# Mixer: convolution and gate tiles as pairs of seven products, the retention output product first, the sums at a phase boundary earlier

## The chip, the cores and the metric

One core of one Trainium2 chip runs one launch of the kernel. The metric is device time in microseconds of that launch; lower is better. TensorE does the matrix products, VectorE and ScalarE the elementwise work, GpSimd (POOL) a little of it and a queue of transfers, SyncE (SP) the queue of weight loads.

## The reference, cut to what matters

One inference step of a two-layer decoder trunk. 512 prompt tokens and 8 x 4 sampled tokens are taken together here: 544 columns. Each layer is a feed-forward block, a mixer, and a second feed-forward block, all with norms before and after. All arithmetic is float32. The mixer, on which the change acts:

```python
proj = u @ w_in                       # 1024 -> 512 q, 512 k, 1024 v, 1024 g, 1024 bg, 1024 cg, 1024 xc, 2048 gates
o = head_rmsnorm(retention(q, k, v, s0))
o_ret = (silu(g) * o) @ w_ret_out     # 1024 x 1024
z = w[0]*full[t] + w[1]*full[t+1] + w[2]*full[t+2]    # full = buffer of 2 rows, then cg * xc
o_conv = (bg * z) @ w_conv_out        # 1024 x 1024
gate_r, gate_c = split(sigmoid(gates))
merged = gate_r * o_ret + gate_c * o_conv
h = h + rmsnorm(merged @ w_o)
```

## The kernel before, in words

Everything is kept transposed: a tile is 128 features x 544 tokens, and 1024 features are KT = 8 tiles. Tokens are worked on in two halves of 272 columns (`hs(0)`, `hs(1)`). A float32 operand is cut into two float32r parts, high and low, and a product is three matmuls: high x high, high x low, low x high (`step`, `mm` on line 321). A *plain job* makes one output tile of 128 features: 8 input tiles x 2 halves x 3 = 48 matmuls into two banks of PSUM. Its weights come by SP's queue into `raw` (three buffers), ScalarE copies the high part (`whi`, line 249), VectorE subtracts the low one (`wlo`, line 253), into 14 buffers, so several jobs ahead.

A *pair* (`Pair`, `run_pair`) makes two output tiles at once. It sees the two weight tiles, each cut in two over its inputs, and the inputs, each tile's two halves of tokens, as 2 x 2 blocks, and does seven block products in place of eight, after a scheme of sums of blocks. A block product is 4 input tiles x 3 = 12 matmuls, so a pair is 84. It uses three banks X, Y, Z. ScalarE copies X into Y (`seed`, line 191) and Z into `p7` (line 392); VectorE forms `Z = Y + p7` (line 395) and `c22 = Y + p7` (line 403) between products, and the last product adds to Y after c22 has been read. The sums of weight blocks are `s_13`, `s_24` (lines 275 to 282, VectorE), cut into parts at lines 260 and 261. The input sums (`ops`: B11, B21, B22, T1 to T4) are made once per phase by `build_ops`, for k = 0 to 3, two feature tiles each; it multiplies x by the gain and the norm's reciprocal r, so the outputs of pairs are normalized already. Before the change, only feed-forward phases have pairs (in parts 2 to 4 of their up product; jobs at `BUILD_AT` call `build_ops`).

A mixer phase before (`mix_jobs`): four heads of six plain jobs (q, k, two v, two g), each head followed by a script of retention work that runs between the steps of later jobs (`retention`, `self.side`, `tick`); three convs of three plain jobs (cg, xc, bg); eight times a gate job (I_GR) and a ret_out job; five more convs; eight times a gate job (I_GC) and a conv_out job; eight wo jobs. The evacuation of plain jobs multiplies by r. Plain jobs' own outputs with r: `ev_gate` line 748, `ev_out` line 754, `ev_cg` 691, `ev_xc` 702, `ev_bg` 723.

The instruction order of TensorE and SP is the order of the program. VectorE, ScalarE and POOL are ordered by a scheduler's priorities, but in a *boundary* between two phases they too follow a script written by hand: `ev(t, fn)` puts fn at planned time t, in us from the start of the next phase's head, and `play` emits all in order of t. The last TAIL = 5 jobs of a phase run half 0 first, then half 1; then the norm's `ry`, the `chain` (scale y, add to x, cut x into `xh` and `xl`, lines 1090 to 1075) per half; then the *head*: the first HEAD = 5 jobs of the next phase, half 0 then half 1, whose banks are copied to SBUF (`copy`, line 1249) since the next norm's r is not known yet. The squares of x are summed into `acc` (`pre_sum`, lines 434 to 443), from planned times `SUMS` = 17.0 and 24.0 on. `rstd` makes r of a half: a matmul with ones (line 464), ScalarE's reciprocal root (476), three instructions of VectorE (477 to 479). `rest(half)` calls rstd and then the evacuations of the five head tiles; it runs from `head_side` as side work after the boundary, at HEAD_REST = 0.5 and 3.2 planned us. The retention script of head 0 begins 4 planned us after the first job behind the head, with `s_transposes` on the tile `stk` (lines 855 to 890).

Activations live in one pool of U_BUFS = 54 buffers of 544 columns (tag u). x is spilled to DRAM (`xd`) and filled again at each boundary, by POOL's queue.

Of the kernel before, what the change touches and what calls it, by code (L numbers as in the profile page):

```python
# [14 lines left out]
DM = 1024  # L15
# [17 lines left out]
BUILD_AT = (6, 9, 11, 13)  # L33
EPS = 1e-6
# [26 lines left out]
SUMS = 17.0, 24.0  # L61
URGENT = 300
HEAD_REST = 0.5, 3.2
# [52 lines left out]
class Pair:  # L116
# [9 lines left out]
    def __init__(self, w1, w2, ops, evac, after=None):  # L126
        self.w1, self.w2, self.ops, self.evac, self.after = w1, w2, ops, evac, after


class Trunk:  # L130
    def __init__(self, ctx, tc, a):
# [10 lines left out]
        self.xd = self.dp.tile([KT, P, NT], F32, tag="xd", name="xd")  # L142
        self.turn, self.given, self.taken = 0, {}, []
# [224 lines left out]
    def run_pair(self, i, j):  # L368

        nc, V = self.nc, self.nc.vector  # L370
        self.prep(i + 1)
        ahead = i + (2 if isinstance(self.jobs[i + 1], Pair) else 1 + LOOK)
# [117 lines left out]
    def ffn_jobs(self, ph):  # L490
# [76 lines left out]
        ph["ops"] = {o: [None] * (KT // 2) for o in ("B11", "B21", "B22", "T1", "T2", "T3", "T4")}  # L567
# [4 lines left out]
    def build_ops(self, ph, k):  # L572
# [5 lines left out]
        for f in (k, k + KT // 2):  # L578
            t = self.u("n")
            V.scalar_tensor_tensor(out=t, in0=self.x[f], scalar=self.gain(l, ph["pre"], f), in1=ph["r"],  # L580
                                   op0=ALU.mult, op1=ALU.mult)
            n.append(t)
            self.spill(f)
        n1, n2 = n
        b11 = self.u("b11", F32R)
        nc.scalar.activation(out=b11[:, A], in_=n1[:, A], func=AF.Copy)
        V.tensor_tensor(out=b11[:, B], in0=n1[:, A], in1=b11[:, A].bitcast(F32), op=ALU.subtract)
# [4 lines left out]
        V.scalar_tensor_tensor(out=t24[:, B], in0=t24[:, A], scalar=-1.0, in1=n2[:, A], op0=ALU.mult, op1=ALU.subtract)  # L592
        b2, p13, p24 = [self.cut((self.u("oh", F32R), self.u("ol", F32R)), t) for t in (n2, t13, t24)]
        for o, hl, s in (("B21", b2, A), ("B22", b2, B), ("T1", p13, A), ("T3", p13, B), ("T2", p24, A), ("T4", p24, B)):
            ph["ops"][o][k] = (hl[0][:, s], hl[1][:, s])
        ph["ops"]["B11"][k] = (b11[:, A], b11[:, B])

# [27 lines left out]
    def mix_jobs(self, ph):  # L625
# [59 lines left out]

        def conv(f):
# [6 lines left out]
            def ev_xc(half, ps):  # L693
                if half == 0:
                    A = st["A"] = self.u("A")
                    S = st["S"] = self.tp.tile([P, NB, 6], F32, tag="as", bufs=2, name=self.name("as"))
                    nc.gpsimd.memset(A[:, 0:2], 0.0)
                    nc.gpsimd.tensor_copy(S[:, :, 0:2], ph["sc"][:, f])
# [5 lines left out]
                if half == 1:  # L704
# [3 lines left out]
                    zs = z[:, SEQ:NT].rearrange("p (b j) -> p b j", j=TS)  # L708
                    cw = [self.cw[:, (l * 3 + i) * KT + f:(l * 3 + i) * KT + f + 1] for i in range(3)]
                    nc.scalar.activation(out=z[:, :SEQ], in_=A[:, 0:SEQ], func=AF.Copy, scale=cw[0])  # L710
                    nc.scalar.activation(out=zs, in_=S[:, :, 0:4], func=AF.Copy, scale=cw[0])
                    for i in (1, 2):
                        nc.vector.scalar_tensor_tensor(out=z[:, :SEQ], in0=A[:, i:i + SEQ], scalar=cw[i],
                                                       in1=z[:, :SEQ], op0=ALU.mult, op1=ALU.add)
                        nc.vector.scalar_tensor_tensor(out=zs, in0=S[:, :, i:i + 4], scalar=cw[i], in1=zs,
                                                       op0=ALU.mult, op1=ALU.add)
                    nc.gpsimd.tensor_copy(ph["cs"][:, f, 0:2], A[:, SEQ:SEQ + 2])
                    nc.gpsimd.tensor_copy(ph["cs"][:, f, 2:18].rearrange("p (b j) -> p b j", j=2), S[:, :, 4:6])

            def ev_bg(half, ps):  # L720
# [4 lines left out]
                if half == 1:  # L725
                    bz[f] = st["z"]
                    if f >= 3:
                        split_bz(f)
# [11 lines left out]
        def out_pair(m, wi, wo, hl, last):  # L740
            st = {}

            def ev_gate(half, ps):
                if half == 0:
                    st["g"] = self.u("gate")
                s = self.hs(half)
                g = st["g"][:, s]
                nc.vector.tensor_tensor(out=g, in0=ps[:, :HALF], in1=ph["r"][:, s], op=ALU.mult)
                nc.scalar.activation(out=g, in_=g, func=AF.Sigmoid)

            def ev_out(half, ps):
                s = self.hs(half)
                g = st["g"][:, s]
                nc.vector.tensor_tensor(out=g, in0=ps[:, :HALF], in1=g, op=ALU.mult)
                if not last:
                    rm[m] = st["g"]
                    return
                if half == 0 and (m < 3 or m == KT - 1):
                    mhl[m] = (self.u("mh", F32R), self.u("ml", F32R))
                nc.vector.tensor_tensor(out=g, in0=rm[m][:, s], in1=g, op=ALU.add)  # L760
                if m in mhl:
                    self.split(*mhl[m], st["g"], s)
                elif half == 1:
                    rm[m] = st["g"]

            return [Job(w[l, wi + m], mv, ev_gate), Job(wo[l, m], lambda: [hl[f] for f in range(KT)], ev_out)]
# [5 lines left out]
        def ready_ret():  # L772
            self.tick(drain=True)
            for f in range(KT):
                split_ret(f)

        def ready_conv():
            for f in range(3):
                split_bz(f)

        def ready_merged():
            for m in range(3, KT - 1):
# [687 lines left out]
```

## Time and profile before

| | |
|---|---|
| time, median of 3 runs | 2715.28 us (2714.5 to 2715.72) |
| the profiled execution: its own time | 2717.34 us |
| its span, first to last instruction | 2715.6 us |
| mean granted clock of TensorE | 0.994 of full speed |
| instructions | 50898 |
| moved by DMA | 283.50 MB, mean 104 GB/s |

All durations below are from the one profiled execution. The times of runs and of the profiled execution hold the launch's ends beside the span. Engines run side by side, so busy times don't add up to the span.

### The profile page before, as it was taken

The numbers are of one execution on the slowest core, as the hardware profiler recorded it, in microseconds if no ns is written. First come the engines' busy times: TensorE is split into PE (matmuls) and PEld (weight loads), VectorE is DVE, ScalarE is ACT, GpSimd is POOL, SyncE is SP. The second block draws the span as 40 slices with busy tenths as digits, with TensorE's granted clock in tenths as the row PEclk, the third lists the DMA queues.
The fourth block names the chain that finished last, engine by engine and source line by source line (L and its number), as shares of the span: only waits on it lengthen the run. The fifth ranks groups of instructions, "written<-read, shape, count | busy, mean of one in ns | idle before, by whom it ended". The sixth has DMA issues, their size and how long they took to land.

```text
span 2715.6 us, 50898 instructions
## 1 busy us (share of the span) xinstructions
PE 2671.4 (98%) x21126; PEld 2658.0 (98%) x21126; DVE 1697.5 (63%) x2995; ACT 1261.2 (46%) x2340; POOL 205.4 (8%) x327
## 2 busy tenths in 40 slices
PE   9999998999999999999999999989999999999998
PEld 9999998999999999999999999989999999999997
DVE  6855757765344368567488657577643443885673
ACT  6555554433222355555565555643432223655553
POOL 1000021121000010000100000211200001000002
PEclk9999999999999999999999999999999999999999
DMA  4233443332222332332332334433322223323332
GB/s 150 90 102 94 132 137 121 105 125 78 93 88 87 94 130 77 101 95 92 128 120 91 93 97 146 140 106 107 114 86 86 90 91 103 105 91 96 102 98 93
DMA packets 88135, 283.50 MB, mean 104 GB/s; under 512 B 11296, under 2 KB 15520, under 8 KB 87904
## 3 DMA queue, kind: packets, MB, share of 16 engines
q1 hardware_dynamic: 74592, 235.46, 28.1%
q0 software_dynamic: 13312, 44.79, 4.8%
q8 instruction: 165, 2.70, 0.4%
q14 instruction: 66, 0.54, 0.1%
HBM read 257.25 MB, written 22.95 MB: 103 GB/s over the span
## 4 chain that ended last, share of the span: by engine, by line
PE 48%; DVE 2%; DMA 1%; ACT 1%; issue 0%; DVEq 0%; ACTq 0%
PE banks L321 46%; DVE wlo L253 0%; ACT whi L249 0%; DMA raw<-in_w_down 0%; DMA raw<-in_w_up 0%; PE banks L464 0%; PE banks L1008 0%; DVE rot L644 0%; ACT sq L437 0%; PE banks L990 0%; PE banks L923 0%; PE banks L1011 0%; DMA raw<-in_w_in 0%; PE banks L969 0%; DVE yg L1119 0%
## 5 line engine op out<-in xcount | busy, mean ns | idle before, releaser
L321 PE MATMUL banks<-xh,whi 128*128 128x272 f32 x2688 | 748.6, 294 | 1.2 <-ACT whi L1313 1.2
L321 PE MATMUL banks<-xl,whi 128*128 128x272 f32 x2688 | 735.8, 289 | 0.0
L249 ACT ACTIVATE whi<-raw 128x1024 fp32r<-128x1024 f32 (+2 forms) x341 | 326.4, 957 | 698.7 <-PE banks L321 477.6
L321 PE MATMUL banks<-xh,wlo 128*128 128x272 f32 x2688 | 596.0, 289 | 0.6 <-DVE wlo L1317 0.4
L321 PEld LDWEIGHTS banks<-xh,whi 128*128 128x128 f32 x2688 | 508.6, 189 | 3.7 <-ACT whi L1313 1.6
L321 PEld LDWEIGHTS banks<-xl,whi 128*128 128x128 f32 x2688 | 508.5, 189 | 1.1
L253 DVE TENSOR_TENSOR wlo<-raw,whi 128x1024 fp32r<-128x1024 f32 (+2 forms) x341 | 374.2, 1099 | 168.9 <-ACT whi L249 143.6
L321 PEld LDWEIGHTS banks<-xh,wlo 128*128 128x128 f32 x2688 | 438.9, 189 | 1.3 <-DVE wlo L1317 0.9
L321 PE MATMUL banks<-oh,whi 128*128 128x272 f32 x1360 | 391.9, 288 | 3.1 <-ACT banks L191 3.0
L321 PE MATMUL banks<-oh,wlo 128*128 128x272 f32 x1360 | 392.1, 288 | 0.0
L321 PE MATMUL banks<-ol,whi 128*128 128x272 f32 x1360 | 390.9, 287 | 0.0
L321 PE MATMUL banks<-hh,whi 128*128 128x272 f32 x1408 | 385.2, 289 | 0.2
L321 PE MATMUL banks<-hl,whi 128*128 128x272 f32 x1408 | 384.4, 288 | 0.4 <-DVE hl L542 0.2
L321 PE MATMUL banks<-hh,wlo 128*128 128x272 f32 x1408 | 313.3, 288 | 0.0
L321 PEld LDWEIGHTS banks<-hl,whi 128*128 128x128 f32 x1408 | 264.9, 188 | 1.0 <-DVE hl L542 0.8
L321 PEld LDWEIGHTS banks<-hh,whi 128*128 128x128 f32 x1408 | 264.9, 188 | 1.0 <-ACT banks L191 0.8
L321 PEld LDWEIGHTS banks<-oh,whi 128*128 128x128 f32 x1360 | 255.8, 188 | 4.2 <-ACT banks L191 4.2
L321 PEld LDWEIGHTS banks<-ol,whi 128*128 128x128 f32 x1360 | 256.3, 188 | 0.0
L321 PEld LDWEIGHTS banks<-oh,wlo 128*128 128x128 f32 x1360 | 255.8, 188 | 0.0
L321 PEld LDWEIGHTS banks<-hh,wlo 128*128 128x128 f32 x1408 | 229.6, 188 | 0.0
L261 DVE TENSOR_TENSOR wlo<-s,whi 128x1024 fp32r<-128x1024 f32 x136 | 166.6, 1225 | 75.2 <-ACT whi L260 39.1
L260 ACT ACTIVATE whi<-s 128x1024 fp32r<-128x1024 f32 x136 | 143.4, 1054 | 41.8 <-DVE s L282 22.2
(233 smaller groups left out, 4332.4 us busy)
## 6 DMA issues: line engine op xcount, KB each, us to landing
raw<-in_w_up SPq DMA_DIRECT2D x173, 512.0 KB, 3.5
raw<-in_w_in SPq DMA_DIRECT2D x128, 512.0 KB, 3.5
raw<-in_w_down SPq DMA_DIRECT2D x96, 320.0 KB, 3.0
raw<-in_w_down SPq DMA_DIRECT2D x32, 448.0 KB, 4.1
xd<-x POOLq DMA_DIRECT2D x40, 272.0 KB, 2.6
x<-xd POOLq DMA_DIRECT2D x40, 272.0 KB, 4.9
s<-in_state_ret POOLq DMA_DIRECT2D x32, 256.0 KB, 3.5
out_ret_s<-s POOLq DMA_DIRECT2D x32, 256.0 KB, 3.0
```

Source lines behind the costliest of these rows:

```text
L249: self.nc.scalar.activation(out=hi[:, :n], in_=r[:, :n], func=AF.Copy)
L253: eng.tensor_tensor(out=lo[:, :n], in0=r[:, :n], in1=hi[:, :n].bitcast(F32), op=ALU.subtract)
L260: self.nc.scalar.activation(out=hi, in_=r, func=AF.Copy)
L261: self.nc.vector.tensor_tensor(out=lo, in0=r, in1=hi.bitcast(F32), op=ALU.subtract)
L321: self.nc.tensor.matmul(out=ps[:, :HALF], lhsT=w, rhs=x, start=start, stop=stop, skip_group_check=again)
```

## The change

The mixer's convs 0 and 1 stay plain (`CONV_PLAIN` = 2). Convs 2 to 7 and all sixteen gate tiles become 17 pairs a layer: a conv pair makes cg and xc of one conv (6), a bg pair makes bg of two convs (3), a gated pair makes the two gates of one m (8). The order of a mixer phase is now: four heads, convs 0 and 1, eight ret_out jobs, three triples (conv pair, conv pair, bg pair), eight times a gated pair and a conv_out job, eight wo jobs. The ret_out outputs are copied to SBUF, stored to a DRAM tensor `od`, and loaded again (`rm`) one gated step ahead. The mixer's ops are built after ret_out jobs 0, 2, 4, 5 (`BUILD_MIX`), with x reloaded from `xd` by POOL's queue; r is no longer multiplied in these evacuations. The splits of seven merged tiles are put together before the last conv_out job. `build_ops` forms t13 and t24 ahead of b11. At every boundary, and at the start, the sums begin earlier (`SUMS` 11.0 and 19.0, 0.45 apart in place of 0.6), one weight preparation moves from 20 to 14, rstd of the two halves is called inside the script at 17.5 and 22.5 (`RSTD_HEAD`), `rest(0)` at 22.6, and `rest(1)` and the spills right after the script.

```diff
@@ -31,6 +31,8 @@
+CONV_PLAIN = 2
+BUILD_MIX = (0, 2, 4, 5)
@@ -58,9 +60,9 @@
-SUMS = 17.0, 24.0
+SUMS = 11.0, 19.0
...
-HEAD_REST = 0.5, 3.2
+RSTD_HEAD = 17.5, 22.5
...
 def log_gammas():
@@ -369,6 +372,8 @@
+        if j.before:
+            j.before()
@@ -564,7 +569,7 @@
-        ph["ops"] = {o: [None] * (KT // 2) for o in ("B11", "B21", "B22", "T1", "T2", "T3", "T4")}
+        self.no_ops(ph)
@@ -577,23 +582,29 @@
-            V.scalar_tensor_tensor(out=t, in0=self.x[f], scalar=self.gain(l, ph["pre"], f), in1=ph["r"],
-                                   op0=ALU.mult, op1=ALU.mult)
+            if ph["kind"] == "mix":
+                nc.gpsimd.dma_start(out=t, in_=self.xd[f])
+            V.scalar_tensor_tensor(out=t, in0=t if ph["kind"] == "mix" else self.x[f],
+                                   scalar=self.gain(l, ph["pre"], f), in1=ph["r"], op0=ALU.mult, op1=ALU.mult)
...
-            self.spill(f)
+            if ph["kind"] != "mix":
+                self.spill(f)
...
-        b11 = self.u("b11", F32R)
-        nc.scalar.activation(out=b11[:, A], in_=n1[:, A], func=AF.Copy)
-        V.tensor_tensor(out=b11[:, B], in0=n1[:, A], in1=b11[:, A].bitcast(F32), op=ALU.subtract)
...
+        b11 = self.u("b11", F32R)
+        nc.scalar.activation(out=b11[:, A], in_=n1[:, A], func=AF.Copy)
+        V.tensor_tensor(out=b11[:, B], in0=n1[:, A], in1=b11[:, A].bitcast(F32), op=ALU.subtract)
...
+    def no_ops(self, ph):
+        ph["ops"] = {o: [None] * (KT // 2) for o in ("B11", "B21", "B22", "T1", "T2", "T3", "T4")}
...
     def spill(self, f):
@@ -683,6 +694,64 @@
+        def conv_tiles(f):
+            A = self.u("A")
+            S = self.tp.tile([P, NB, 6], F32, tag="as", bufs=2, name=self.name("as"))
+            nc.gpsimd.memset(A[:, 0:2], 0.0)
+            nc.gpsimd.tensor_copy(S[:, :, 0:2], ph["sc"][:, f])
+            return A, S
+        def short_conv(f, A, S, z):
...
+        def conv_pair(f):
+            st = {}
+            def ev(tile, half, c):
+                s = self.hs(half)
+                if tile == 0:
+                    if half == 0:
+                        st["c"] = self.u("cg")
+                    nc.scalar.activation(out=st["c"][:, s], in_=c, func=AF.Copy)
+                    return
+                if half == 1:
+                    st["A"], st["S"] = conv_tiles(f)
+                A, S, t = st["A"], st["S"], st["c"][:, s]
+                n = HALF if half == 0 else SEQ - HALF
+                nc.vector.scalar_tensor_tensor(out=A[:, 2 + half * HALF:2 + half * HALF + n], in0=c[:, :n], scalar=-1.0,
+                                               in1=t[:, :n], op0=ALU.mult, op1=ALU.mult)
+                if half == 1:
+                    nc.vector.scalar_tensor_tensor(out=S[:, :, 2:6], in0=c[:, n:].rearrange("p (b j) -> p b j", j=TS),
+                                                   scalar=-1.0, in1=t[:, n:].rearrange("p (b j) -> p b j", j=TS),
+                                                   op0=ALU.mult, op1=ALU.mult)
+                else:
+                    bz[f] = self.u("z")
+                    short_conv(f, A, S, bz[f])
+            return Pair(w[l, I_CG + f], w[l, I_XC + f], lambda: ph["ops"], ev)
+        def bg_pair(f):
+            def ev(tile, half, c):
+                z = bz[f + tile][:, self.hs(half)]
+                if tile == 0:
+                    nc.vector.tensor_tensor(out=z, in0=c, in1=z, op=ALU.mult)
+                else:
+                    nc.vector.scalar_tensor_tensor(out=z, in0=c, scalar=-1.0, in1=z, op0=ALU.mult, op1=ALU.mult)
+                if half != tile:
+                    split_bz(f + tile)
+            return Pair(w[l, I_BG + f], w[l, I_BG + f + 1], lambda: ph["ops"], ev)
         def conv(f):
@@ -724,8 +780,6 @@
-                    if f >= 3:
-                        split_bz(f)
@@ -737,33 +791,46 @@
-        def out_pair(m, wi, wo, hl, last):
+        def ret_out(m):
...
-            def ev_gate(half, ps):
+            def ev(half, ps):
...
-                    st["g"] = self.u("gate")
-                s = self.hs(half)
-                g = st["g"][:, s]
-                nc.vector.tensor_tensor(out=g, in0=ps[:, :HALF], in1=ph["r"][:, s], op=ALU.mult)
-                nc.scalar.activation(out=g, in_=g, func=AF.Sigmoid)
+                    st["o"] = self.u("o")
+                nc.scalar.activation(out=st["o"][:, self.hs(half)], in_=ps[:, :HALF], func=AF.Copy)
+                if half == 1:
+                    nc.gpsimd.dma_start(out=self.od[m], in_=st["o"])
+            return Job(a["w_ret_out"][l, m], lambda: [rhl[f] for f in range(KT)], ev)
+        def load_o(m):
+            if m < KT:
+                rm[m] = self.u("o")
+                nc.gpsimd.dma_start(out=rm[m], in_=self.od[m])
+        def gated(m):
+            st = {}
+            def ev(tile, half, c):
+                if half == tile:
+                    st[tile] = self.u("gate")
+                nc.scalar.activation(out=st[tile][:, self.hs(half)], in_=c, func=AF.Sigmoid, scale=1.0 - 2.0 * tile)
+                if (tile, half) == (0, 1):
+                    nc.vector.tensor_tensor(out=rm[m], in0=rm[m], in1=st[0], op=ALU.mult)
...
             def ev_out(half, ps):
...
-                g = st["g"][:, s]
+                g, x = st[1][:, s], rm[m][:, s]
...
-                if not last:
-                    rm[m] = st["g"]
-                    return
-                if half == 0 and (m < 3 or m == KT - 1):
+                if half == 0 and m == KT - 1:
...
-                nc.vector.tensor_tensor(out=g, in0=rm[m][:, s], in1=g, op=ALU.add)
-                if m in mhl:
-                    self.split(*mhl[m], st["g"], s)
-                elif half == 1:
-                    rm[m] = st["g"]
-            return [Job(w[l, wi + m], mv, ev_gate), Job(wo[l, m], lambda: [hl[f] for f in range(KT)], ev_out)]
+                nc.vector.tensor_tensor(out=x, in0=x, in1=g, op=ALU.add)
+                if m == KT - 1:
+                    self.split(*mhl[m], rm[m], s)
+            return [Pair(w[l, I_GR + m], w[l, I_GC + m], lambda: ph["ops"], ev, before=lambda: load_o(m + 1)),
+                    Job(a["w_conv_out"][l, m], lambda: [bzhl[f] for f in range(KT)], ev_out)]
...
         def square_r():
@@ -771,15 +838,16 @@
         def ready_ret():
...
+            self.of_mix(False)
...
         def ready_conv():
-            for f in range(3):
+            for f in range(CONV_PLAIN):
...
         def ready_merged():
-            for m in range(3, KT - 1):
+            for m in range(KT - 1):
@@ -796,20 +864,27 @@
-        for f in range(3):
+        for f in range(CONV_PLAIN):
...
+        jobs += [ret_out(m) for m in range(KT)]
+        jobs[first].before = ready_ret
+        self.no_ops(ph)
+        for k, at in enumerate(BUILD_MIX):
+            jobs[first + at].after = lambda k=k: self.build_ops(ph, k)
+        first = len(jobs)
+        for f in range(CONV_PLAIN, KT, 2):
+            jobs += [conv_pair(f), conv_pair(f + 1), bg_pair(f)]
+        jobs[first].after = ready_conv
+        def after_conv():
+            out_states()
+            load_o(0)
+        jobs[-1].after = after_conv
...
-            jobs += out_pair(m, I_GR, a["w_ret_out"], rhl, False)
-        jobs[first].before = ready_ret
-        first = len(jobs)
-        for f in range(3, KT):
-            jobs += conv(f)
-        jobs[first].before = ready_conv
-        jobs[-1].after = out_states
-        for m in range(KT):
-            jobs += out_pair(m, I_GC, a["w_conv_out"], bzhl, True)
+            jobs += gated(m)
@@ -1102,7 +1177,7 @@
-                ev(SUMS[half] + 0.6 * f, lambda f=f: self.pre_sum(nxt, f, half, None, nc.vector))
+                ev(SUMS[half] + 0.45 * f, lambda f=f: self.pre_sum(nxt, f, half, None, nc.vector))
...
     def finish(self, ev, ph, d):
@@ -1207,7 +1282,7 @@
-                           (20.0, 21.0)):
+                           (14.0, 15.0)):
@@ -1256,7 +1331,6 @@
         def rest(half):
...
-            self.rstd([nxt["acc"][:, self.hs(half)]], half, nxt["r"], DM)
@@ -1266,12 +1340,16 @@
+        for half in range(2):
+            ev(RSTD_HEAD[half], lambda half=half: self.rstd([nxt["acc"][:, self.hs(half)]], half, nxt["r"], DM))
+        ev(RSTD_HEAD[1] + 0.1, lambda: rest(0))
...
     def head_side(self, nxt):
-        self.side = [(self.clock + HEAD_REST[half], lambda half=half: nxt["rest"](half)) for half in range(2)]
+        nxt["rest"](1)
...
-            self.side += [(self.clock + HEAD_REST[1] + 0.1 * (f + 1), lambda f=f: self.spill(f)) for f in range(KT)]
+            for f in range(KT):
+                self.spill(f)
...
     def begin(self, ph):
```

## Rows read from the trace of the kernel before

**Rows 1.** page, busy us of each engine (share of the span), xinstructions

```profile
PE 2671.4 (98%) x21126; PEld 2658.0 (98%) x21126; DVE 1697.5 (63%) x2995; ACT 1261.2 (46%) x2340; POOL 205.4 (8%) x327
```

**Rows 2.** waits of TensorE: engine line <- releaser: us in total, times, longest

```profile
PE banks L890 <- DVE stk L860: 14.1, 2, 7.0
PE banks L464 <- DVE acc L443: 8.8, 5, 2.1
```

**Rows 3.** tiles rh and bh, matmuls: ns min/median/max, first to last start

```profile
L321 PE MATMUL banks<-rh,whi x256: 284/289/293, 651.6 to 2089.2; 128*128 128x272 f32 x128
...
L321 PE MATMUL banks<-bh,whi x256: 283/288/293, 837.9 to 2276.0; 128*128 128x272 f32 x128
```

**Rows 4.** windows: length, then each engine's busy us (xinstructions), PEclk, DMA, GB/s

```profile
651.60:837.90 186.30, 186.30 (x1491) 186.30 (x1490) 79.19 (x136) 48.41 (x67) 3.94 (x21) 1.00 0.29 90
```

**Rows 5.** timeline of ScalarE, p7 copies (start us, us, instruction, [idle before])

```profile
280.67 0.37 ACT L392 ACTIVATE p<-banks 128x272 f32<-128x272 f32 x1
...
322.89 0.37 ACT L392 ACTIVATE p<-banks 128x272 f32<-128x272 f32 x1
```

**Rows 6.** groups of VectorE, 280.67 to 333.37: busy us, mean ns | idle before

```profile
L261 DVE TENSOR_TENSOR wlo<-s,whi 128x1024 fp32r<-128x1024 f32 x10 | 12.2, 1225 | 1.9 <-ACT whi L260 1.4
...
L542 DVE TENSOR_TENSOR hl<-g,hh 128x544 fp32r<-128x544 f32 x5 | 3.6, 725 | 1.9 <-ACT hh L541 1.4
L261 DVE TENSOR_TENSOR v<-raw,v 128x512 fp32r<-128x512 f32 x5 | 3.5, 692 | 1.7 <-ACT v L260 1.7
...
L275 DVE TENSOR_TENSOR s<-raw,raw 128x512 f32<-128x512 f32 x4 | 2.7, 681 | 0.0
...
L537 DVE SCALAR_TENSOR_TENSOR g<-c,g 128x272 f32<-128x272 f32 x5 | 2.2, 434 | 0.0
```

**Rows 7.** windows, one pair of a feed-forward phase

```profile
208.44:219.00 10.56, 10.56 (x86) 10.56 (x85) 8.91 (x14) 5.58 (x11) 0.00 (x0) 1.00 0.28 81
```

**Rows 8.** groups of VectorE, 609.3 to 645.4 (plain convs, layer 0)

```profile
L713 DVE SCALAR_TENSOR_TENSOR z<-A,cw,z 128x512 f32<-128x512 f32 x4 | 3.0, 742 | 0.0
L484 DVE TENSOR_TENSOR rl<-sg,rh 128x544 fp32r<-128x544 f32 x4 | 2.6, 712 | 0.0
...
L715 DVE SCALAR_TENSOR_TENSOR z<-as,cw,z 128x32 f32<-128x32 f32 x4 | 1.0, 240 | 0.0
...
L702 DVE TENSOR_TENSOR A<-banks,cg 128x272 f32<-128x272 f32 x2 | 0.9, 442 | 4.0 <-PE banks L321 4.0
```

**Rows 9.** timeline of VectorE, end of the last head of layer 0

```profile
620.05 1.36 DVE L1040 TENSOR_TENSOR sg<-sg,rh 128x544 f32<-128x544 f32 x2
```

**Rows 10.** page, DMA issues: xcount, KB each, us to landing

```profile
x<-xd POOLq DMA_DIRECT2D x40, 272.0 KB, 4.9
```

**Rows 11.** timeline of TensorE, head of the first mixer and half 1's norm

```profile
384.43 0.28 PE L321 MATMUL banks<-xh,whi 128*128 128x272 f32 x1
...
390.04 0.62 PE L464 MATMUL banks<-yacc,ones 128*128 128x272 f32 x2
```

**Rows 12.** timeline of VectorE, same boundary

```profile
392.56 0.79 DVE L1090 TENSOR_TENSOR yg<-y,ry 128x272 f32<-128x272 f32 x2
...
402.48 0.50 DVE L1075 SCALAR_TENSOR_TENSOR xl<-x,par,xh 128x272 fp32r<-128x272 f32 x1 [0.18 <-ACT xh L1069]
...
419.71 0.44 DVE L443 SCALAR_TENSOR_TENSOR acc<-sq,acc 128x272 f32<-128x272 f32 x1
...
422.50 0.44 DVE L666 TENSOR_TENSOR v<-out,r 128x272 f32<-128x272 f32 x1
...
427.36 0.43 DVE L646 TENSOR_TENSOR k<-k,rot 128x272 f32<-128x272 f32 x1
...
436.72 0.21 DVE L860 TENSOR_TENSOR stk<-kz,stk 128x64 fp32r<-128x64 f32 x1
```

**Rows 13.** windows, the stop at stk and after it

```profile
429.90:437.00 7.10, 0.06 (x2) 0.01 (x1) 6.92 (x24) 1.81 (x3) 0.00 (x0) 0.86 0.23 75
437.00:441.70 4.70, 4.70 (x21) 4.70 (x22) 4.34 (x12) 1.26 (x4) 0.00 (x0) 0.50 0.35 113
```

More of the change, by code (lines that the diff above doesn't have):

```diff
@@ L116, with __init__ @@
 class Pair:
-    def __init__(self, w1, w2, ops, evac, after=None):
-        self.w1, self.w2, self.ops, self.evac, self.after = w1, w2, ops, evac, after
+    def __init__(self, w1, w2, ops, evac, before=None, after=None):
+        self.w1, self.w2, self.ops, self.evac, self.before, self.after = w1, w2, ops, evac, before, after
 class Trunk:
@@ L142, in __init__ @@
         self.xd = self.dp.tile([KT, P, NT], F32, tag="xd", name="xd")
+        self.od = self.dp.tile([KT, P, NT], F32, tag="od", name="od")
         self.turn, self.given, self.taken = 0, {}, []
@@ L684, in head @@
                     Job(w[l, I_G + 2 * h], mv, ev_g(0)), Job(w[l, I_G + 2 * h + 1], mv, ev_g(1), after=go)]
+        def conv_tiles(f):
[5 more added lines that the diff above has]
+        def short_conv(f, A, S, z):
+            zs = z[:, SEQ:NT].rearrange("p (b j) -> p b j", j=TS)
+            cw = [self.cw[:, (l * 3 + i) * KT + f:(l * 3 + i) * KT + f + 1] for i in range(3)]
+            nc.scalar.activation(out=z[:, :SEQ], in_=A[:, 0:SEQ], func=AF.Copy, scale=cw[0])
+            nc.scalar.activation(out=zs, in_=S[:, :, 0:4], func=AF.Copy, scale=cw[0])
+            for i in (1, 2):
+                nc.vector.scalar_tensor_tensor(out=z[:, :SEQ], in0=A[:, i:i + SEQ], scalar=cw[i],
+                                               in1=z[:, :SEQ], op0=ALU.mult, op1=ALU.add)
+                nc.vector.scalar_tensor_tensor(out=zs, in0=S[:, :, i:i + 4], scalar=cw[i], in1=zs,
+                                               op0=ALU.mult, op1=ALU.add)
+            nc.gpsimd.tensor_copy(ph["cs"][:, f, 0:2], A[:, SEQ:SEQ + 2])
+            nc.gpsimd.tensor_copy(ph["cs"][:, f, 2:18].rearrange("p (b j) -> p b j", j=2), S[:, :, 4:6])
@@ L694, in ev_xc @@
                 if half == 0:
[L695 to L698, printed above, removed]
+                    st["A"], st["S"] = conv_tiles(f)
                 A, S = st["A"], st["S"]
@@ L707, in ev_xc @@
                     z = st["z"] = self.u("z")
[L708 to L718, printed above, removed]
+                    short_conv(f, A, S, z)
             def ev_bg(half, ps):
```

## The prediction, on record before the result

> **What bounds the kernel now.** I read the page's table of engines first: TensorE is busy for 98% of the span, VectorE for 63% and ScalarE for 46% [rows 1]. So a microsecond counts if TensorE is spared it or made to wait for it, and not otherwise. The waits of TensorE come next: 14.1 us in two stops before the first head's transposes, held by the tile stk of VectorE, and 8.8 us in five stops at the ones-matmul of a norm, held by the sum of squares acc [rows 2]. Then its pace in the two kinds of job. Between the first ret_out matmul of a layer (651.6) and the first conv_out matmul (837.9) lie 31 plain jobs of 48 matmuls: 186.3 us / 1488 = 0.1252 us a matmul [rows 3], with TensorE busy throughout and VectorE for 79 of the 186 us [rows 4]. A seven-product pair, as the feed-forward phases have it, copies p7 once; from 280.67 to 322.89 there are four pairs: 10.555 us each for 84 matmuls, 0.1257 us apiece [rows 5]. Pairs therefore run at the pace of plain jobs, and fewer matmuls are less time.
>
> **Part 1, seven products for eight.** Two plain tiles take 96 x 0.1252 = 12.02 us, a pair 10.555. That spares 1.465 us, in 17 pairs of each of two layers: 34 x 1.465 = **49.8 us off**. The eight ret_out jobs are only moved, and the gates of the retention half now lie in the pairs. The Trainium skill (TensorE: Matmul & The Clock Gate, Back-to-back issue gap) gives a lone warm matmul N/2.4 + 2.5 ns, 115.8 ns at 272 columns; the trace disagrees with 125.2. By that page of the Trainium skill the 12 matmuls of a pair would be worth 1.39 us and this part 47.2; the row decides.
>
> **Part 2, the work beside it.** A pair costs VectorE more than two plain tiles. In the feed-forward a pair's instructions are three low parts of 1.225, one of 0.69, four additions of 0.68, two combinations in a bank and, as its evacuation, two products, all four of 0.43, and a low part of 0.725 [rows 6]: 9.53 us by their durations, and 8.91 us of VectorE in a pair of 10.56, since records overlap a little [rows 7]. I scale by 8.91/9.53 = 0.935. In the mixer the evacuation (1.585) is replaced. For a conv pair: two products with cg (0.44), two long and two short taps (0.74, 0.24), some 0.2 for the sample columns: 3.0 us [rows 8], so 10.98 x 0.935 = 10.3 us. For a bg pair: four products with z (0.44) and two splits (0.71): 3.2, so 10.4 us. A triple of two conv pairs and one bg pair is then 31.0 us of VectorE in 31.7 of TensorE, 98%. The gated stage (a pair and a conv_out job, 16.6 us) needs about 11, and is safe.
>
> The cover in the triples is thin but real: VectorE still fits, and weights are prepared about a pair ahead. What can be late is the in-order pair of combinations: TensorE waits in a pair's last product for the read of the bank by the combination c22, which has one product (12 x 0.1257 = 1.5 us) to be done, behind an instruction of up to 1.23 us. Six conv pairs and three bg pairs a layer make 18. Below: nothing, as in the feed-forward, where no wait of this kind shows among the long ones. Above: VectorE keeps the 1.65 us that it idles in a feed-forward pair (10.56 - 8.91) on top of its new work: 10.3 + 1.65 - 10.56 = 1.4 us in each of 18, 25 us. I take 5, nearer to the feed-forward, since much of that idling is only being ahead.
>
> The ret_out jobs follow one another now and begin after two convs, not three and a gate. They take 8 x 6.01 = 48 us. VectorE has the four builds there (each two scalings, five half-tile operations, three low parts, some 5.5 us), eight splits (5.7), the weights of the plain jobs (8 x 1.23) and of the first pair (7.1): about 43 of 48 us. The head's last norm product ends near 621.4 [rows 9]; with one conv and the gate less the first ret_out comes near 627.6 (651.6 - 24), and takes its eight inputs 0.75 us apart, while a split costs 0.71. It begins with some 6 us in hand and two short evacuations beside it. Below nothing, above 4 us a layer; I take 1. The last build follows job 5 and has two jobs, 12 us, before the first pair; its two reloads from memory land 4.9 us after issue [rows 10]. Below nothing; above, one landing and one build, 10 us a layer. I take 0.5 a layer, and as much for the seven splits now put together before conv_out 7 (7 x 0.71 = 5 us under a job of 6). Stores and loads of o are 16 transfers of 272 KB a layer on POOL's queue, where nothing on TensorE's path waits but rm, loaded one gated step (16.6 us) ahead: nothing, or one landing of 4.9 a layer if that cover went. New waits in the mixer: 5 + 2 + 1 + 1 = **9 us on**.
>
> **Part 3, the boundary.** The head of the mixer starts at 384.43 [rows 11]; its second half 15.0 + 0.6 us later, 400.1. The norm of half 0 now stands behind four of eight steps, about 404.6, that of half 1 behind 96 matmuls of that half, about 412.7. VectorE runs the second chain of x nearly without a gap, 392.56 to 402.98 [rows 12]: 24 instructions and a weight part of 1.2, 0.38 us apiece. The earlier sums (seven) and the earlier weight part go in among it, so the last xl is at 402.98 + 2.7 + 1.2 = 406.9 instead; TensorE wants it at 400.1 + 0.6 + 63 x 0.1257 = 408.6. That hides the move, with 1.7 us to spare; without this cover the lateness counts in full in each of five heads. Sum 0 is done five such instructions and a weight part before that, 403.8; sum 1 after a norm's tail (three) and seven more, 410.7; both before the matmuls that need them. So the five stops of 8.8 us go; I leave 0.5 us in each for arriving late: **6.3 off** (bounds 0 and 8.8).
>
> The stop at stk: VectorE finished acc at 420.15 and stk at 436.9, with both norms' tails and the evacuation of ten half tiles between, 5.3 us a half (422.50 to 427.79) [rows 12]. TensorE idled for 7.0, and its granted clock read 0.50 (1.2 GHz) for the 4.7 us after: 21 matrix instructions where about 37 fit at 2.4 GHz, 2.1 us more [rows 13]. So each stop costs 9.1, both 18.3. After: a norm takes 2.5 us from its matmul at 390.04 to the first use at 392.56 [rows 11, 12], so r of half 1 is there at 415.2; two evacuations, 425.8; then one job's evacuation, two weight parts and stk (0.9 + 2.4 + 0.8), 429.9. TensorE, without its stop at acc, comes at 428.4. New beside it: the first evacuation's Silu now stands on ScalarE ahead of the copies that empty banks of half 1, so the first job after the head can wait some 0.9 us for a bank, and comes 0.9 later. Left: 0.9 + 0.8 a layer, with the clock as it was before the stop. **14.9 off** (bounds 0 and 18.3). The start and the other boundaries change only in order.
>
> **Sum.** 2717.3 - 49.8 - 6.3 - 14.9 + 9 = 2655.3, against the profiled execution. The median of the runs is 2.1 lower, so **2653 us** timed. A difference of 0.2% (5.4 us) is about what the measurement can tell from none.
>
> **Rivals.** *VectorE sets the pace in the triples.* For it: 98% by the sum, and an in-order queue; against it: weights ready a pair ahead. At 1.4 us a pair, 25 instead of 5: 2673 us. Chance 0.14.
> *The boundary waits only move.* The sums sit in a chain that VectorE already runs without a gap; if xl or the acc of half 0 comes late, or stk stays behind the weight parts, the 21.2 us stay: 2674. Against: 1.7 us to spare for xl, and both norms now end before the head does, without a table load of ScalarE between their evacuations. Chance 0.12.
> *No new waits at all.* As the feed-forward pairs: 2644. It lies in my range; chance 0.17.
> *The other side: operands come too late.* At the last build, 16 split tiles of ret, 32 operands and temporaries, r, two z and two o are 53 of the pool's 54 buffers. If a reload must wait for a buffer that the last ret_out job frees, each build runs alone in front of the first pair. It decides from 64 us, 32 a layer: three landings and builds in series (3 x 10.4) with TensorE idle and half a clock after. For it: 53 of 54; against: three builds can be over before the last job, so only one can be caught, 10 us a layer. 2673 with one, 2717 or more with all. Chance 0.03 for slower, 0.02 for no change.
> The forecast with its small waits keeps 0.52. The cases up to 2674 hold the rest, so I give **2640 to 2676**: below, no new waits and nothing left of the boundary's, 2638; above, one rival in full. Faster 0.95, same 0.02, slower 0.03.
>
> **What would show it.** Right: 408 fewer matmuls of the weights; p7 copies 10.5 to 10.8 us apart in the triples; no wait of TensorE for acc; at stk under 2 us, the granted clock staying at 2.4 GHz there; VectorE at 93% or more in the triples. Wrong: waits of matmuls for c22 or for weights' low parts in most of the 18 pairs; a stop of 5 us or more between ret_out 7 and the first pair; waits for xl in the heads.

## The result and the profile after

The changed kernel took 2679.83 us (median of four runs, 2677.17 to 2681.31) beside 2714.89 for the kernel before on the same chip: a ratio of 0.9866, 95% interval 0.9853 to 0.988. It is 35 us faster, not 62, and 4 us above the upper end of the range. The profiled execution took 2677.17 us with a span of 2675.3, against 2717.3 and 2715.6 before.

The page's engine rows after the change:

```profile
PE 2628.3 (98%) x20718; PEld 2606.1 (97%) x20718; DVE 1861.0 (70%) x3213; ACT 1354.0 (51%) x2546; POOL 237.3 (9%) x375
```

Against [rows 1] TensorE has 21126 - 20718 = 408 matmuls fewer, exactly the 34 pairs' worth. So the first term was done, and the missing microseconds are, in the main, waits. The waits of TensorE after (total us, times, longest), as [rows 2] before:

```profile
PE banks L469 <- DVE acc L448: 15.4, 10, 1.6
PE banks L324 <- ACT out L1324: 8.7, 6, 2.8
...
PE banks L324 <- DVE rl L489: 1.5, 2, 0.7
PE banks L324 <- ACT o L800: 1.0, 1, 1.0
```

The stop at stk is gone, as forecast. But acc, which should have gone as well, stops TensorE ten times where it did five, and a new line stands behind it: the copies `out` by which ScalarE empties the head's banks, 8.7 us in 6 stops. All lines of the list together come to 32.7 us; before they came to 31.1. The boundary's waits moved.

Where this lies is seen from the first ones-matmul of each phase's output norm (tile yacc), the same instruction in both traces: 372.38, 962.94, 1342.42, 1719.98, 2311.53 and 2689.93 us before, 375.44, 941.15, 1321.85, 1700.68, 2269.24 and 2649.70 after. The stretches between them changed by +3.1 (start and first feed-forward), **-24.8** (boundary and mixer), +1.2, +1.3 (feed-forwards), **-23.0** (the second mixer) and +2.1.

The boundary that [rows 12] show before, VectorE after the change:

```profile
402.11 0.44 DVE L444 TENSOR_TENSOR acc<-acc,sq 128x272 f32<-128x272 f32 x1 [0.78 <-ACT sq L442]
...
404.52 0.99 DVE L444 TENSOR_TENSOR acc<-acc,sq 128x272 f32<-128x272 f32 x2 [0.50 <-ACT sq L442]
...
408.67 0.44 DVE L448 SCALAR_TENSOR_TENSOR acc<-sq,acc 128x272 f32<-128x272 f32 x1 [0.75 <-ACT sq L442]
...
409.80 1.22 DVE L256 TENSOR_TENSOR wlo<-raw,whi 128x1024 fp32r<-128x1024 f32 x1
...
411.70 1.22 DVE L256 TENSOR_TENSOR wlo<-raw,whi 128x1024 fp32r<-128x1024 f32 x1
412.83 0.50 DVE L1150 SCALAR_TENSOR_TENSOR xl<-x,par,xh 128x272 fp32r<-128x272 f32 x1
...
418.77 0.43 DVE L448 SCALAR_TENSOR_TENSOR acc<-sq,acc 128x272 f32<-128x272 f32 x1
```

and ScalarE in the same stretch:

```profile
403.65 0.53 ACT L1144 ACTIVATE xh<-x,par 128x272 fp32r<-128x272 f32 x1 [1.24 <-DVE x L1169]
404.08 1.06 ACT L442 ACTIVATE sq<-x 128x272 f32<-128x272 f32 x3
406.25 0.53 ACT L1144 ACTIVATE xh<-x,par 128x272 fp32r<-128x272 f32 x1 [1.12 <-DVE x L1169]
406.68 0.41 ACT L442 ACTIVATE sq<-x 128x272 f32<-128x272 f32 x1
...
423.47 1.28 ACT L687 ACT_TABLE_LOAD   x1
424.76 0.43 ACT L687 ACTIVATE sg<-sg 128x272 f32<-128x272 f32 x1
425.10 1.24 ACT L1324 ACTIVATE out<-banks 128x272 f32<-128x272 f32 x4
```

Read the brackets across the two fences. ScalarE waits 1.24 us for VectorE's new x before it can make xh; the squares stand behind that xh in its queue; VectorE waits 0.50 us for those squares before it can go on to the next x, for which ScalarE then waits 1.12 us. Two engines that each have idle time take turns. The second chain takes 17.6 us, from 395.70 (its first yg) to 413.3 (the last xl), where it took 10.4 before [rows 12]; VectorE was busy for 15.3 of the 17.6 and waited for 2.3, where it waited for 0.2 before. So most of the added 7.2 us is VectorE's own work put into the chain (the seven sums, and the two weight parts at 409.80 and 411.70), and 2.1 us are waits of this kind. This boundary stands 3.1 us later than before's, so the last xl, forecast for 406.9, is 3.3 us late beyond that shift; acc of half 1, forecast for 410.7, comes at 419.2, 5.4 late. TensorE's stops at the end of it, with what released it:

```profile
419.26 0.72 PE L469 MATMUL banks<-acc,ones 128*128 128x272 f32 x2 [1.60 <-DVE acc L448]
...
425.53 0.39 PE L324 MATMUL banks<-xh,whi 128*128 128x272 f32 x1 [2.29 <-ACT out L1324]
```

The second of them waits for the copies of 425.10, which had stood behind the table load and the Silu of 423.47 to 425.10 (and these behind a weight split that had waited 1.42 us for its transfer). Of the 8.7 us of such stops, 2.52, 2.29 and 2.83 fall at the start and in the two mixers; the three feed-forward heads have 0.28 to 0.40 each. Behind two of these stops TensorE's granted clock is at 1.2 GHz for a while, in the first feed-forward (stop until 48.96) and in the second mixer (until 1751.24); columns as [rows 4]:

```profile
49.50:52.90 3.40, 3.40 (x17) 3.40 (x17) 3.40 (x11) 2.71 (x7) 0.00 (x0) 0.50 0.00 0
1752.70:1756.10 3.40, 3.40 (x17) 3.40 (x16) 3.34 (x10) 0.30 (x1) 0.00 (x0) 0.50 0.00 0
```

The same window 49.50 to 52.90 of the kernel before holds 29 matrix instructions, at 2.4 GHz.

### The profile page after: what moved, and what is told of

It is laid out like the page before. It is cut to its first block, busy times and chain, and to the rows that moved or that the text cites. A ratio compares the mean times of both kernels' runs of the same rounds, so it can differ in the third digit from the quotient of the medians.

```text
span 2675.3 us, 50606 instructions
## 1 busy us (share of the span) xinstructions
PE 2628.3 (98%) x20718; PEld 2606.1 (97%) x20718; DVE 1861.0 (70%) x3213; ACT 1354.0 (51%) x2546; POOL 237.3 (9%) x375
## 5 line engine op out<-in xcount | busy, mean ns | idle before, releaser
L324 PE MATMUL banks<-oh,whi 128*128 128x272 f32 x2040 | 588.6, 289 | 3.0 <-ACT banks L194 1.6
L324 PE MATMUL banks<-oh,wlo 128*128 128x272 f32 x2040 | 587.9, 288 | 0.0
L324 PE MATMUL banks<-ol,whi 128*128 128x272 f32 x2040 | 586.6, 288 | 0.0
L324 PE MATMUL banks<-xh,whi 128*128 128x272 f32 x1600 | 455.2, 298 | 9.6 <-ACT out L1324 8.7
L324 PE MATMUL banks<-xl,whi 128*128 128x272 f32 x1600 | 442.4, 289 | 0.0
L324 PEld LDWEIGHTS banks<-ol,whi 128*128 128x128 f32 x2040 | 384.5, 188 | 0.0
L324 PE MATMUL banks<-xh,wlo 128*128 128x272 f32 x1600 | 371.5, 289 | 0.4 <-DVE wlo L1395 0.4
L324 PEld LDWEIGHTS banks<-xh,whi 128*128 128x128 f32 x1600 | 303.4, 190 | 13.2 <-ACT out L1324 10.0
L324 PEld LDWEIGHTS banks<-xl,whi 128*128 128x128 f32 x1600 | 303.4, 190 | 2.1 <-DVE xl L1150 1.0
L324 PEld LDWEIGHTS banks<-xh,wlo 128*128 128x128 f32 x1600 | 267.9, 190 | 1.1 <-DVE wlo L1395 1.1
```

What stands on the lines that cost most here:

```text
L324: self.nc.tensor.matmul(out=ps[:, :HALF], lhsT=w, rhs=x, start=start, stop=stop, skip_group_check=again)
```

## The experiments

Times are medians; the kernel before took 2715.7 to 2716.5 beside them. Each ratio is to that kernel, with its 95% interval.

**1 and 2. Each half alone.** The changed kernel with the boundary as it was:

```
-SUMS = 11.0, 19.0
-RSTD_HEAD = 17.5, 22.5
+SUMS = 17.0, 24.0
+HEAD_REST = 0.5, 3.2
-                           (14.0, 15.0)):
+                           (20.0, 21.0)):
...
+            self.rstd([nxt["acc"][:, self.hs(half)]], half, nxt["r"], DM)
...
-            ev(RSTD_HEAD[half], lambda half=half: self.rstd([nxt["acc"][:, self.hs(half)]], half, nxt["r"], DM))
-        ev(RSTD_HEAD[1] + 0.1, lambda: rest(0))
...
-        nxt["rest"](1)
+        self.side = [(self.clock + HEAD_REST[half], lambda half=half: nxt["rest"](half)) for half in range(2)]
```

> The pairs and the new order of the mixer, with the whole boundary as it was before the change. Theory A (the pairs bring about 49.8 - 9 = 41 us as forecast, and the boundary change, against the forecast, brings nothing: ten stops at acc of 1.7 and 9 us of stops behind ScalarE's copies take the place of two stops at stk): 2674 to 2683 us, with two stops of about 7 us at stk and five at acc in the waits of TensorE. Theory B (the boundary brings its 21 us and the pairs only half of theirs): about 2700 us.

2676.57 us, 0.9858 (0.9844 to 0.9873): 39.2 us off. Its waits are those of before:

```profile
PE banks L965 <- DVE stk L935: 12.6, 2, 7.0
PE banks L469 <- DVE acc L448: 9.2, 5, 2.5
```

Its two mixer stretches are 20.2 and 20.6 us shorter than before's, its others -0.5, -1.7, +1.1 and -0.8. And the kernel before with the boundary's edits alone (the same lines the other way round):

> The kernel before with the boundary changed alone: earlier sums, norms inside the script, first evacuation behind them. Theory A: within 4 us of the kernel before (2711 to 2717), ten stops at acc of about 1.7 us, some 9 us behind copies, none at stk. Theory B: 2694 us.

2720.62 us, 1.0017 (1.0008 to 1.0027): 4.9 us **on**, by the medians, outside theory A's 2711 to 2717 and far from theory B's 2694; the two profiled spans differ by 0.5.

```profile
PE banks L464 <- DVE acc L443: 15.5, 10, 1.6
PE banks L321 <- ACT out L1249: 8.9, 6, 2.8
```

So the two lines of the result belong to the boundary's edits. By the starts of the same norms it takes 3.6 and 4.1 us off the two mixer stretches and adds 3.2 in the first stretch and 1.5, 1.2 and 2.4 in the feed-forwards, where there was no stk to gain. The halves add up: -39.2 + 4.9 = -34.3, and both together gave -35.1.

**3. Norms and evacuation later.** The first evacuation behind all copies, against the changed kernel:

```
-RSTD_HEAD = 17.5, 22.5
+RSTD_HEAD = 21.5, 25.1
-        ev(RSTD_HEAD[1] + 0.1, lambda: rest(0))
+        ev(28.0, lambda: rest(0))
```

> The changed kernel with the norm of half 0 behind all eight steps of the head's second half (planned 21.5 for 17.5), that of half 1 behind the whole head (25.1 for 22.5), and the first evacuation behind the copies of the banks (28.0 for 22.6). Theory A: the stops at acc (15 us) and behind the copies (9 us) go and the time is 2655 to 2661 us, unless stk comes late again. Theory B: TensorE is not held by them, 2678 to 2682 us.

2671.71 us, 0.9838 (0.9823 to 0.9853): 8 us better than the change, 11 above the upper end that I expected. The norms, no longer asked for early, left the late xl to be seen, and stk came back:

```profile
PE banks L324 <- DVE xl L1150: 8.0, 13, 1.1
PE banks L965 <- DVE stk L935: 6.9, 2, 3.5
PE banks L469 <- DVE acc L448: 2.8, 2, 1.7
```

**4. The evacuation alone later.** The norms stay where the change has them:

```
-        ev(RSTD_HEAD[1] + 0.1, lambda: rest(0))
+        ev(28.0, lambda: rest(0))
```

> The changed kernel with only the first evacuation moved behind the copies of the banks (28.0 for 22.6). Theory A: the stops behind copies go (9 us), those at acc stay: about 2671 us. Theory B: 2678 to 2682 us.

2669.1 us, 0.9828 (0.9813 to 0.9842): 10.7 us better. All six stops at the copies are gone, acc stays as it was:

```profile
PE banks L469 <- DVE acc L448: 15.4, 10, 1.6
```

That settles the first evacuation, with its Silu and its table load: where nothing else moved, keeping it behind the copies was worth the 8.7 us listed and 2 more. In this run the two stretches at half clock behind those stops are gone too.

**5 and 8. The sums behind the chain.** The fifth run, against the fourth, moves the sums, the norms and the later weight preparation; the eighth, against the third, the sums and nothing else (its first two lines).

```
-SUMS = 11.0, 19.0
+SUMS = 17.0, 19.5
-RSTD_HEAD = 17.5, 22.5
+RSTD_HEAD = 22.3, 25.1
-                           (14.0, 15.0)):
+                           (20.0, 21.0)):
```

> The changed kernel with the squares and sums of both halves behind the second chain (due 17.0 and 19.5 us after the boundary's zero, not 11.0 and 19.0), the norms at 22.3 and 25.1, the bank evacuation at 28.0 and the weight preparation back at 20.0 and 21.0. Theory A (the squares queued inside the chain make VectorE and ScalarE wait for each other in turn; the work itself has room): no stop for acc at the ones matmul, none at the copies, under 1 us per boundary for xl, at most 2 us at each stk: 15 us of the listed PE waits fall to under 8, and the time is 2652 to 2661. Theory B (there is more VectorE and ScalarE work before the head than time for it, and every order only moves the stop): the listed waits at the head's lines keep 13 to 18 us together, and the time is 2667 to 2674.

2670.88 us, 0.9836 (0.982 to 0.9852). Missed: no stop for xl, but 15.6 us for acc in five stops of up to 3.2. ScalarE's timeline of that run says what held the sums now:

```profile
411.93 1.06 ACT L252 ACTIVATE whi<-raw 128x1024 fp32r<-128x1024 f32 x1 [2.86 <-DMA raw<-in_w_in]
...
415.37 0.41 ACT L442 ACTIVATE sq<-x 128x272 f32<-128x272 f32 x1
```

A weight's split waits 2.86 us for its transfer, and the last square stands behind it in the queue.

> The third experiment (norms at 21.5 and 25.1, evacuation at 28.0: 2671.7) with the sums alone moved behind the chain, to 17.0 and 19.5. Theory A (the squares inside the chain make xl late): the 8.0 us at L1150 fall under 2, stk keeps at most 7: 2660 to 2667. Theory B (the order only moves the stop): 2669 to 2674, with as much wait at the head's lines as before.

2661.85 us, 0.98 (0.9785 to 0.9815): 9.9 us better than the third run by the one line. The 8.0 us at xl are gone:

```profile
PE banks L469 <- DVE acc L448: 7.9, 5, 2.1
PE banks L324 <- ACT banks L194: 3.0, 4, 1.7
PE banks L965 <- DVE stk L935: 2.2, 2, 1.1
```

Its second chain runs from 392.00 to 405.2, and the windows view of that stretch shows VectorE busy for 12.91 of 13.20 us: no taking of turns is left. The one line took both out of the chain, VectorE's work on the sums and the waits between the engines; the run does not price them apart.

**6. Fewer pairs.** The fourth run with three pairs a layer less:

```
-CONV_PLAIN = 2
+CONV_PLAIN = 4
```

> The changed kernel with the evacuation at 28.0 (the fastest so far, 2669.1) and four plain convolution tiles in each mixer layer, not two: three pairs less a layer, six in all, 144 + ... 72 more matmuls. Theory A (a pair saves its 12 matmuls, about 1.5 us, less 0.25 us that VectorE's copies now cost it): plus 6 x 1.2 = 7.3 us, 2675 to 2678. Theory B (in the triples VectorE sets the pace, and a pair there saves little): plus 0 to 3 us, 2669 to 2672.

2675.16 us, 0.985 (0.9835 to 0.9865): 6.1 us more than the fourth run, 1.0 us a pair. Nearer to theory A, under its 7.3. But the pairs that were left ran faster. Two of ScalarE's p7 copies in that run, three pairs apart:

```profile
730.17 0.40 ACT L397 ACTIVATE p<-banks 128x272 f32<-128x272 f32 x1 [0.84 <-PE banks L324]
...
761.69 0.40 ACT L397 ACTIVATE p<-banks 128x272 f32<-128x272 f32 x1 [1.11 <-PE banks L324]
```

10.51 us a pair, where three of the changed kernel take 32.36 us, 10.79 each.

**7. The weight preparation back.** The fourth run with the later preparation where it was before the change:

```
-                           (14.0, 15.0)):
+                           (20.0, 21.0)):
```

> The changed kernel with the evacuation at 28.0 and the one later weight preparation back at 20.0 and 21.0 (not 14.0 and 15.0). Theory A (the squares alone make the lag): acc's stops at the ones matmul stay within 3 us of 15.4 in 10, 2667 to 2671. Rival (the preparation's VectorE steps of about 1 us each ahead of the chain's end make it): acc's stops fall by 5 us or more, and the time is 2662 to 2665.

2665.72 us, 0.9817 (0.9802 to 0.9831). My theory A, that the squares alone make the lag, falls; the rival's mechanism holds, its time just missed:

```profile
PE banks L469 <- DVE acc L448: 7.7, 10, 1.2
```

Half of the acc stops came from that one preparation having been moved ahead of the sums. The gain was 3.4 us (the runs of the two kernels overlap, 2667.4 to 2669.8 and 2664.6 to 2668.3) for 7.7 us of stops, since stops at l (4.7 us in 2) and stk (2.0) came up behind.

**9 to 12. All sums together, and then the evacuation.** The ninth is the eighth run with the sums ahead of the split that waits; the tenth is the ninth with the preparation at 20.0 and 21.0, as in the seventh; the eleventh and twelfth are the ninth with the first evacuation at 23.5 and at 25.0.

```
-SUMS = 17.0, 19.5
+SUMS = 15.2, 17.4
...
-        ev(28.0, lambda: rest(0))
+        ev(23.5, lambda: rest(0))
```

> The eighth experiment (2661.9) with the sums due at 15.2 and 17.4, not 17.0 and 19.5: still behind the chain, but now ahead of the weight split that waited 2.58 us for its transfer on ScalarE with the last three squares queued behind it. Theory A (what stands ahead of the squares in ScalarE's queue sets the sums, and nothing else is short): the 7.9 us in 5 stops for acc fall under 2, 2652 to 2657. Theory B (the boundary is full, the stop goes elsewhere): the same 15 us of listed waits, 2660 to 2664.

2659.01 us, 0.979 (0.9776 to 0.9803). acc is gone from the list, but the first line is now

```profile
PE banks L965 <- DVE stk L935: 9.5, 2, 4.8
```

Both theories are half right. The three feed-forward stretches are 3.2, 3.1 and 2.6 us shorter than before's; in the mixers the stop moved on.

> The ninth experiment with the later weight preparation back at 20.0 and 21.0, behind the sums. Theory A: it keeps VectorE 1.2 us freer ahead of the sums, and nothing waits for it: within 2 us of the ninth, under 2 us of waits for acc. Rival (as in the fifth, its wait for a transfer holds the norm behind it): the acc stops stay gone, but the norm and the copies come later, 3 to 8 us more than the ninth.

2662.93 us, 0.98 (0.9786 to 0.9813): 3.9 us more than the ninth by the medians, with runs that overlap, as the rival said; stk 11.8 us.

> The ninth experiment (2659.0) with the first half's evacuation due at 23.5, not 28.0: ahead of the second norm, in the 4 us in which VectorE waited for weight transfers and the second norm while the first norm was ready at 414.1. Theory A (the order of the queues sets what is late, and this is the order in which the data come): the two stops of 4.8 us for stk fall under 1.5 each, none for acc, at most 2 us in all for the bank copies behind the table load: 2649 to 2654. Theory B (the work of the boundary fills it, so one stop always remains): 2656 to 2662, with 8 us or more listed at the head's lines.

2658.07 us, 0.9786 (0.9773 to 0.9799): no different from the ninth, and theory B. stk still takes 8.0 us in 2. The windows view of this boundary, from the sums to the first transposes (columns as [rows 4]):

```profile
405.00:432.00 27.00, 23.12 (x180) 22.62 (x179) 26.24 (x61) 18.35 (x33) 1.64 (x3) 1.00 0.58 188
```

VectorE is busy for 26.24 of the 27.00 us. The idle time that I had meant to fill is filled, with weights' low parts that now come earlier: six stand ahead of stk where five did, and stk, counted from the first ones-matmul of this boundary, comes only 0.8 us sooner. The edit also brought table loads of ScalarE, 41 in the eleventh and twelfth runs for 29 in the ninth.

> The same with the evacuation due at 25.0, between the copies of the second half's first three banks and the second norm. Theory A: within 2 us of the run with 23.5, with less wait for the copies. Theory B: 2656 to 2662.

2658.28 us, 0.9784 (0.9771 to 0.9798): as the eleventh, stk 8.2 us. The ninth, eleventh and twelfth beat both kernels, by some 58 us the one and 21 the other.

## Why the prediction was wrong

**Parts 1 and 2 were right.** -49.8 + 9 = -40.8 was forecast; the pairs alone gave -39.2 by the medians, and -20.2 and -20.6 in the two mixer stretches. The 9 us of new waits were of about the right size but partly in other places, so that the total agrees is in part luck. In the changed kernel's triples the p7 copies lie 10.79 us apart, 0.23 above the feed-forward's pace [rows 5]:

```profile
710.13 0.40 ACT L397 ACTIVATE p<-banks 128x272 f32<-128x272 f32 x1 [1.06 <-PE banks L324]
...
742.49 0.40 ACT L397 ACTIVATE p<-banks 128x272 f32<-128x272 f32 x1 [1.06 <-PE banks L324]
...
774.86 0.40 ACT L397 ACTIVATE p<-banks 128x272 f32<-128x272 f32 x1 [1.02 <-PE banks L324]
```

18 x 0.23 = 4.2 us, where I took 5. The wait that I named is there, but not in each of the 18: TensorE's weight loads wait for c22 (tile c; total, times, longest, over the whole kernel)

```profile
PEld banks L324 <- DVE c L408: 4.4, 16, 0.4
```

six times in the triples, once in each, some 2.1 us of the 4.2; the other ten lie in the gated steps and the feed-forwards. VectorE is busy 92% in the stretch, one point under the 93% that I had set as the sign:

```profile
720.00:770.00 50.00, 49.74 (x392) 49.08 (x390) 46.00 (x78) 28.46 (x44) 7.71 (x19) 1.00 0.39 123
```

The gated steps, which I called safe, cost as much: from 825.09 to 875.65 three of them take 16.85 us each, not 16.57, in gaps of 0.1 us, three a step (one behind c22, two at the copy of X into Y): 16 x 0.28 = 4.5 us for which I had nothing. The start of ret_out (rl and o, 2.5 us) was taken at 2, and it came at 625.6 (forecast 627.6). For the last build and for the merged splits, taken at 1 each, no stop shows. (VectorE's work beside ret_out adds up to 44.6 us and not to about 43, which changes nothing here.) The rival of the triples (1.4 us a pair) is refuted. With one triple a layer fewer, in the sixth run, the pairs looked at ran at 10.51, so the 0.23 us is not the pair's own; which neighbour in VectorE's queue makes it, no run separates.

**The step that failed is Part 3: "both before the matmuls that need them".** I made the times of the sums and of xl from VectorE's work alone, 24 instructions and a weight part at 0.38 us apiece, and added the moved ones to it. The sums are fed by ScalarE, which I gave no line. The chain was to take 14.3 us and took 17.6. Of the 3.3 us too many, 2.1 are VectorE's waits for ScalarE's squares, and 1.2 a second weight part: the trace has two low parts more in the chain than before, where I had charged one. Experiments 3 and 8 differ in the place of the sums only, and 9.9 us lie between them. Experiments 4 and 7 differ in the moved weight preparation only, and half of the acc stops lie between them; it takes both low parts out of the chain (14.8 us in the seventh run) and a split of 1.05 us that ScalarE makes ahead of the last square of half 0. The forecast of -6.3 for acc became five stops more: 6.6 us of listed waits on, not 6.3 off.

**"The start and the other boundaries change only in order" failed with it.** I had seen the Silu ahead of the copies and put 0.9 us on it, in the mixers alone. It stops every head: 8.7 us in 6, 2.8 at the longest and 7.6 of it at the start and in the mixers. In the mixers ScalarE's queue held not only the Silu but a table load of 1.28 us, behind a weight split that came late with its transfer; at the start ScalarE waited between the pieces of the evacuation for VectorE. Experiment 4 is the proof that the place of the evacuation makes these stops.

**The stk stop went as forecast**, and with it the slow clock behind it. (TensorE at 428.4 + 0.9 and stk at 429.9 leave 0.6 us and not the 0.8 of the sum.) The stretch that [rows 13] show at half clock, after:

```profile
437.00:441.70 4.70, 4.70 (x41) 4.70 (x40) 4.61 (x9) 2.06 (x5) 0.00 (x0) 1.00 0.83 246
```

41 matrix instructions, at a granted clock of 2.4 GHz, where there were 21 at 1.2. The listed 14.1 us and the 4.2 of the clock went, and 6.6 + 8.7 us came in their place, with two new stretches at half clock: 17 matrix instructions in 3.4 us where 29 fit, some 1.4 us each by that count, 2.9 in all. That is 18.3 us off and 18.2 on. The rival "the boundary waits only move" named this, at 2674 and with a chance of 0.12, and the upper end of the range was set by it. By the medians the boundary's edits cost 4.9 us more than that rival, which had them at nothing. The listed waits of experiment 2 (31.8 us in all) and its span account for under 1 of these 4.9. Its profiled execution was the fastest of its ten runs, 2.7 us under their median, and that of the kernel before was some 2 above its own; what makes the runs of one kernel differ by this no trace tells, and it stays open.

How far the order alone could have gone, the later runs show: 2658, near the 2653 forecast, with acc and the copies settled. They come near it by another order than the forecast's, so they do not bear it out. What is left is the stop at stk, and there the eleventh run found VectorE full. Part 3 had TensorE arriving there at 428.4 and stk at 429.9; in that run stk came at 432.1, with 4.0 us of stop and not 0.8, and the granted clock at half for 3.4 us behind it (432.2 to 435.6). That another split of the work (a weight part of 1.22 us on another engine) would remove it was not tried.

## What to carry to other kernels

When work is moved into a chain that runs without a gap, draw it on every engine that feeds it, in queue order: two engines that each have room can still wait for one another in turn. Here such hand-overs were 2.1 of the 7.2 us by which the chain grew, and VectorE's added work the rest. Ask of each instruction that is put ahead what it itself may wait for (a transfer, a table load), because everything behind it in that queue inherits the wait. And where a boundary occurs in several kinds of phase, price the move in each: here two mixers gained about 4 us apiece, and the start and three feed-forward phases gave it back.

## What the runs showed of the hardware

The load of an activation table took 1.28 us in each of these traces, and the next instruction began 0.01 us after it (423.47 + 1.28, and 424.76). The Trainium skill (ScalarE: Activation LUTs, What ACT_TABLE_LOAD costs) gives about 1283 ns for the load, with which the trace agrees, and some 1380 ns of drain besides; in this trace the split ahead of the load ended at 423.45, so no such drain shows here.

A transfer that is late held up work that did not need it: the weight splits on ScalarE waited 2.58 to 2.86 us for raw in the fifth and eighth runs, and in the eighth run the squares behind one of them started at 413.49, though the last x had been ready since 402.84.
